# Token-major products that run from the last column to the first, with the split weights at a place that differs by chunk

## The chip, the core and the metric

One core of a Trainium2 chip runs the whole kernel in one launch. The metric is the device time in microseconds (us); the times shown are medians over runs of the same program on the same kind of core. The profile is that of one execution.

## What is computed

One decoder layer on 256 tokens of width 2048, in float32. Cut to what matters here:

```
proj = h @ w_in[l]                            # 2048 x 6144: q, k, v of 8 + 8 heads
a_out = diff_attention(q_d, k_d, v_d, ...)    # 8 heads
b_out = moba_attention(q_m, k_m, v_m, ...)    # 8 heads
mix = concatenate([a_out, b_out]) @ w_out[l]  # 2048 x 2048
h = layer_norm(DEEPNORM_ALPHA * h + mix, ...)
u = h @ w_up                                  # 2048 x 11264: gate and value
f = (silu(causal_dwconv3(gate)) * value) @ w_down   # 5632 x 2048
h = layer_norm(DEEPNORM_ALPHA * h + f, ...)
```

Nearly all of the arithmetic is in the products with the four weight matrices.

## The kernel before, in words

**Three products for one.** TensorE multiplies in a reduced float32 form (`F32R`). To keep the precision, every operand is split into a part `hi`, the value rounded to that form, and a part `lo`, the rest. A product is then hi x hi + hi x lo + lo x hi. ScalarE (ACT) writes `hi` and VectorE (DVE) subtracts to get `lo`: `split` (line 165), `split_hi` and `split_lo` (lines 187 and 197), `split_first` (line 203).

**Two directions.** A matmul holds a stationary operand of 128 x 128 in the array and streams a moving operand of up to 512 columns past it, into one of eight banks of 512 float32 columns. In the *feature-major* products (queries, keys, gate and value; `mm_feature`, line 284, and `up_products`, line 1291) the weights are stationary, and the activations move: 512 columns, hi and lo of 256 tokens, against the `hi` weights, then 256 columns against the `lo` weights. In the *token-major* products (values, output projection, down projection) 128 tokens of the activations are stationary and 512 columns of the weights move, three products for each. These are `mm_token` (line 298), `mm_count` (line 718), through which `mm_d`, `mm_pair`, `mm_three` and the products of `down_products` go, and `mm_d_end` (line 1537), with 256 columns.

**Where the moving operands lie.** The weights come in chunks of 128 x 2048, listed in `stream` and numbered by `i`: 16 of kind "v" (values), 32 of "q" and "k", 16 of "o" (output projection), 88 of "g" and "u" (gate and value), and some of "d" (down projection). Each is loaded by DMA some chunks ahead, and each half of it (1024 columns) is split into one tile `hi` and one tile `lo` of the pool `splits`, six buffers each. Such a tile has 1088 columns, of which 1024 are used. For "v", "o", "d" and the first gate and value chunk, the used part begins 8 columns (32 bytes) into the tile, and for the others at 0: the constant `MOVE_AT`. As the program lays out memory, these tiles begin 96 bytes into a block of 256 bytes, so that the used part begins at 128 with the shift, and at 96 without. The other large operands begin at 128: the activations `x` and `h` in split form, the attention's outputs `mh` and `ml`, and the tiles of block sums named below. One small tile, `hl`, begins at 0.

**Chunks with seven products.** Some chunks are multiplied by a scheme that needs seven block products and some block sums in place of eight (`mm_seven`, line 747). Its operands are sums of blocks of weights in tiles with fixed places: `vhi` and `vlo`, `oslot`, `slot`, and for the early part of the down projection `tslot` and `rslot`, with sums of activations as stationary operands (`wh`, `wl`, `hh`, `hl`, `sp`, `more`, `back`).

**The order.** It is written out by hand. TensorE goes through the chunks; while it works on chunk i, ACT and DVE split chunk i+2, and SP issues the load of a chunk five or six further on. In the stage of gate and value, products of the down projection are put between the chunks (`up_step`, line 1375: `up_products`, then the work of ACT and DVE, then a slice of `down_products`). The value projection takes the first 90 us, queries, keys and attention go to 296, the output projection to 400, gate, value and early down products to 1054, and the remaining down projection and the last norm to the end.

Of the kernel before, what the change touches and what calls it, by code (L numbers as in the profile page):

```python
# [12 lines left out]
F32R = mybir.dt.float32r  # L13
# [3 lines left out]
P = 128  # L17
# [41 lines left out]
MOVE_AT = 8  # L59
# [3 lines left out]
def hymba_layer(ctx: ExitStack, tc: tile.TileContext, a: dict):  # L63
# [3 lines left out]
    def pool(name, bufs=1, space=None):  # L67
        kw = {} if space is None else {"space": space}
        return ctx.enter_context(tc.tile_pool(name=name, bufs=bufs, **kw))

    keep = pool("keep")
    splits = pool("splits", 6)
# [8 lines left out]
    loaded, parts, waiting = {}, {}, {}  # L81

    stream = []
# [23 lines left out]
    first_u = next(i for i, s in enumerate(stream) if s[0] == "g")  # L107
    first_d = next(i for i, s in enumerate(stream) if s[0] == "d")

    def pieces(i, half=None):  # L110

        cuts = [0, 2048] if half is None and stream[i][0] != "v" else [0, 1024, 2048]
        both = [(x, y) for x, y in zip(cuts, cuts[1:])]
        return [p for p in both if half is None or p[0] // 1024 == half]

    def rows_of(p, x, y):
        return 2 * p + x // 512, 2 * p + y // 512
# [42 lines left out]
    def by_dma(i, half):  # L160

        kind, h, _, _ = stream[i]
        return kind == "k" and h < NDIFF and half == 1

    def split(i, half, both=None):

        if i >= NS or (i, half) in parts:
            return
        t = loaded[i] if half == 0 else loaded.pop(i)
        if both is None:  # L170
            o = MOVE_AT if stream[i][0] in "vod" or i - first_u in (0, 1) else 0
            hi, lo = (splits.tile([P, 1088], F32R, name=n)[:, o:o + 1024] for n in ("hi", "lo"))
        else:
            hi, lo = both[:, half], both[:, 2 + half]
        for x, y in pieces(i, half):
            if stream[i][0] == "v" and stream[i][2] == half == 0:
                split_x(*rows_of(stream[i][1], x, y))
            s = slice(x - 1024 * half, y - 1024 * half)
            if by_dma(i, half):
                ACT.activation(lo[:, s], t[:, x:y], AF.Copy, scale=-1.0)  # L180
                POOL.dma_start(lo[:, s], t[:, x:y], accum_op=ALU.add)
            ACT.activation(hi[:, s], t[:, x:y], AF.Copy)  # L182
            if not by_dma(i, half):
                DVE.tensor_tensor(lo[:, s], t[:, x:y], hi[:, s].bitcast(F32), ALU.subtract)  # L184
        parts[i, half] = (hi, lo)

    def split_hi(i, half):
        if i >= NS or (i, half) in parts:
            return
        o = MOVE_AT if stream[i][0] in "vod" or i - first_u in (0, 1) else 0  # L190
        hi, lo = (splits.tile([P, 1088], F32R, name=n)[:, o:o + 1024] for n in ("hi", "lo"))
        t = loaded[i] if half == 0 else loaded.pop(i)
        ACT.activation(hi, t[:, half * 1024:half * 1024 + 1024], AF.Copy)  # L193
        parts[i, half] = (hi, lo)
        waiting[i, half] = t
# [7 lines left out]
    def split_first(i):  # L203

        t = loaded.pop(i)
        for c in range(2):
            parts[i, c] = tuple(splits.tile([P, 1088], F32R, name=n)[:, MOVE_AT:MOVE_AT + 1024] for n in ("hi", "lo"))
        for k in range(2):
            split_x(2 * i + k, 2 * i + k + 1)
            for c in range(2):  # L210
                hi, lo = (x[:, k * 512:k * 512 + 512] for x in parts[i, c])
                src = t[:, c * 1024 + k * 512:c * 1024 + k * 512 + 512]
                ACT.activation(hi, src, AF.Copy)  # L213
                DVE.tensor_tensor(lo, src, hi.bitcast(F32), ALU.subtract)

    def weights(i, x, w):

        hi, lo = parts[i, x // 1024]
        return hi[:, x % 1024:x % 1024 + w], lo[:, x % 1024:x % 1024 + w]
# [11 lines left out]
    def split_x(k0, k1):  # L231
        t = xraw[:, k0 * S:k1 * S].rearrange("p (k t) -> p k t", t=S)
        ACT.activation(xh[:, k0:k1], t, AF.Copy)
        DVE.tensor_tensor(xl[:, k0:k1], t, xh[:, k0:k1].bitcast(F32), ALU.subtract)
# [46 lines left out]
    def mm(out, lhsT, rhs, start, stop):  # L281
        PE.matmul(out, lhsT, rhs, start=start, stop=stop)  # L282
# [14 lines left out]

    def mm_token(dst, i, x, ah, al, first, last):

        w = [weights(i, x + c * 512, 512) for c in range(len(dst))]  # L300
        for c, d in enumerate(dst):
            mm(d, ah, w[c][0], first, False)
        for c, d in enumerate(dst):
            mm(d, ah, w[c][1], False, False)
        for c, d in enumerate(dst):
            mm(d, al, w[c][0], False, last)


    heads = {}
# [404 lines left out]
    MB = {1: bank[4], 5: bank[5], 6: bank[6], 7: bank[7]}  # L714
    MO = ({1: bank[7], 5: bank[5], 6: bank[6], 7: bank[4]}, {1: bank[3], 5: bank[0], 6: bank[2], 7: bank[1]})
    counts, total = {}, {}

    def mm_count(key, dst, lhs, rhs):

        n = counts[key] = counts.get(key, 0) + 1  # L720
        if key in total:
            mm(dst, lhs, rhs, n == 1, n == total[key])

    def mm_three(key, dst, lhs, rhs):
        for x, y in ((0, 0), (0, 1), (1, 0)):
            mm_count(key, dst, lhs[x], rhs[y])

    def mm_d(i, t, cs, k):

        kind, _, n, _ = stream[i]  # L730
        ts = slice(t * P, (t + 1) * P)
        ah, al = (x[:, ts] for x in aparts[i, k])
        w = [weights(i, 1024 * c + 512 * k if kind == "v" else (1536 * c if k == 0 else 512 + 512 * c), 512) for c in cs]
        for lhs, j in ((ah, 0), (ah, 1), (al, 0)):
            for c, wc in zip(cs, w):
                mm_count((kind, n, t, c), CB[t][c], lhs, wc[j])
# [171 lines left out]
    for i in range(2):  # L908
        split_first(i)
        load(4 + i)  # L910
    split(2, 0)

    def begin(i):

        urgent(i)
        j = i + 2
        if j < NS and seven(j):
            blocks_raw(j)
            act_sums(j)
        elif j - 1 < NS and seven(j - 1):  # L920
            blocks_sum(j - 1, 1)
            if j - 1 >= VP:
                split(j, 1)
            blocks_hi(j - 1, 1)
            if j - 1 < VP:
                blocks_whole(j - 1)
                blocks_lo(j - 1, 3)
            else:
                blocks_lo(j - 1, 3)
                blocks_whole(j - 1)  # L930
            if j - 1 < VP:
                split(j, 0)
                split(j, 1)
        else:
            split(j, 0)
            split(j, 1)
        if i >= first_d:
            act_back(i + 3)
        load(i + 6)
        pending(i)  # L940
# [138 lines left out]
    def mm_o(i, kk, t):  # L1079
        _, half, j, _ = stream[i]  # L1080
        ts = slice(t * P, (t + 1) * P)
        h = 2 * j + kk
        mm_token(bank[4 * half + 2 * t:4 * half + 2 * t + 2], i, kk * 1024, head(0, h)[:, ts], head(1, h)[:, ts],
                 h == 0, h == NH - 1)

    def mm_o_columns(i, t, c):
        _, half, j, _ = stream[i]
        ts = slice(t * P, (t + 1) * P)
        for kk in range(2):
            h = 2 * j + kk  # L1090
            mm_token([bank[4 * half + 2 * t + c]], i, (kk * 2 + c) * 512, head(0, h)[:, ts], head(1, h)[:, ts],
                     h == 0, h == NH - 1)
# [17 lines left out]
    last = range(first_u - PAIRED, first_u)  # L1110
    for i in range(first_o, last[0]):
# [23 lines left out]
        n, j = stream[i][1:3]  # L1135
# [239 lines left out]
    def up_step(i):  # L1375
# [25 lines left out]
        if carried:  # L1401
            carried.pop()()
        split_hi(i + 2, 0)
        behind = 0 <= turning < SEGMENTS - 1 and step == 3
        if 2 in now and behind:
# [23 lines left out]
        if 0 in new:  # L1429
            s_lo(1)  # L1430
        split_hi(i + 2, 1)
        if behind:
            up_copy(i)
# [96 lines left out]
    last = range(NS - PAIRED_END, NS)  # L1530
# [6 lines left out]
    def mm_d_end(j):  # L1537

        for i in last:
            for k in range(2):  # L1540
                wh, wl = weights(i, 1536 - 512 * k + j * 256, 256)
                ah, al = (x[:, P:2 * P] for x in aparts[i, k])
                dst = MB[5 + j][:, 0:256]
                mm(dst, ah, wh, i == last[0] and k == 0, False)
                mm(dst, ah, wl, False, False)
                mm(dst, al, wh, False, i == last[-1] and k == 1)
# [3 lines left out]
    for i in range(first_d, NS - PAIRED_END):  # L1550
        begin(i)
        _, p, n, j = stream[i]
# [102 lines left out]
    for j in range(2):  # L1655
        mm_d_end(j)
        z_piece(1, 6 + j, MB[5 + j][:, 0:256], 2, 256, 1.0)
        if j == 0:
            z_times_g(1)
# [94 lines left out]
```

## Time and profile before

| | us |
|---|---|
| median of 3 runs | 1105.75 (1105.56 to 1106.29) |
| span of the profiled execution, first to last instruction | 1104.2 |
| TensorE busy with products (PE) | 1094.6, 5884 products |
| TensorE busy with loading stationary operands (PEld) | 943.7 |
| VectorE (DVE) | 947.3 |
| ScalarE (ACT) | 720.5 |
| GpSimd (POOL) | 71.6 |

The profile gives the span of its execution and no other time for it; the median lies 1.55 us above this span. "Line 282" is the helper through which all products go, so the groups are told apart by the names in them: `bank<-hi,x` has the moving operand `hi` and the stationary operand `x`, and `bank<-x,hi` the other way about. Products overlap: one that lasts 390 ns in a row can be followed by the next after 227 ns, and the distance between starts is the one that adds up to the span.

### The profile page before, as it was taken

The page shows a single profiled execution, that of the slowest core. Times are in us where ns is not written, and L with a number is a line of the kernel's source. Part 1 is how long each engine was busy: PE and PEld are TensorE (multiplying, and loading weights), DVE is VectorE, ACT ScalarE, POOL GpSimd, SP SyncE. Part 2 cuts the span into 40 slices and gives each one's busy share as a digit, 9 for nine tenths or more (in the row PEclk, how much of TensorE's full clock was granted, in tenths as well). Part 3 has the DMA queues.
Part 4 walks back from the last instruction along what each step waited for, and adds up shares of the span by engine and source line. Part 5 has one row for each costly group of instructions (what it writes and reads, how often), then busy time and mean ns, then how long its engine had stood idle before and what let it go on. Part 6 is the DMA issues. An engine that isn't in the chain of part 4 may idle for free.

```text
span 1104.2 us, 16138 instructions
## 1 busy us (share of the span) xinstructions
PE 1094.6 (99%) x5884; PEld 943.7 (85%) x5884; DVE 947.3 (86%) x1613; ACT 720.5 (65%) x1166; POOL 71.6 (6%) x99
## 2 busy tenths in 40 slices
PE   9999999999999999999999999999999999999997
PEld 6888888888888898888888888888888888888886
DVE  6987778888789879888999989998899988998776
ACT  6765676655475386666667767676776767677652
POOL 0100110000000000000000000000100000000003
PEclk9999999999999999999999999999999999999999
DMA  9799876444468647888888889889888889888672
GB/s 338 262 284 304 259 214 209 155 153 153 163 200 260 226 151 233 288 274 270 311 276 285 296 283 326 298 311 308 280 271 280 306 309 300 302 278 282 205 293 77
DMA packets 64336, 283.54 MB, mean 257 GB/s; under 512 B 6576, under 2 KB 8064, under 8 KB 46464
## 3 DMA queue, kind: packets, MB, share of 16 engines
q1 hardware_dynamic: 53456, 235.57, 57.5%
q0 software_dynamic: 10656, 46.67, 19.0%
q8 instruction: 46, 0.75, 0.3%
q14 instruction: 34, 0.28, 0.1%
q10 hardware_dynamic: 144, 0.26, 0.1%
HBM read 233.69 MB, written 20.97 MB: 231 GB/s over the span
## 4 chain that ended last, share of the span: by engine, by line
PE 94%; DVE 3%; ACT 1%; issue 0%; DMA 0%; SPq 0%; POOL 0%; ACTq 0%; DVEq 0%
PE bank L282 94%; PE bank L428 0%; DMA raw<-in_w_v 0%; DVE lo L201 0%; DVE tslot L844 0%; ACT tslot L841 0%; DVE z L1365 0%; ACT hi L193 0%; DVE z L1150 0%; ACT rslot L1514 0%; DVE st L499 0%; DVE rslot L1516 0%; PE bank L1159 0%; PE bank L475 0%; DVE z L496 0%
## 5 line engine op out<-in xcount | busy, mean ns | idle before, releaser
L282 PE MATMUL bank<-h,hi 128*128 128x512 f32 x1376 | 481.0, 390 | 0.2 <-ACT ub L1279 0.2
L282 PE MATMUL bank<-h,lo 128*128 128x256 f32 x1376 | 387.9, 282 | 0.0
L282 PEld LDWEIGHTS bank<-h,hi 128*128 128x128 f32 x1376 | 258.3, 188 | 55.1 <-ACT ub L1279 0.6
L282 PEld LDWEIGHTS bank<-h,lo 128*128 128x128 f32 x1376 | 260.0, 189 | 3.6
L201 DVE TENSOR_TENSOR lo<-raw,hi 128x1024 fp32r<-128x1024 f32 x171 | 208.2, 1220 | 16.1 <-ACT hi L193 15.9
L282 PE MATMUL bank<-x,hi 128*128 128x512 f32 x512 | 182.9, 398 | 0.0
L193 ACT ACTIVATE hi<-raw 128x1024 fp32r<-128x1024 f32 x171 | 178.6, 1048 | 0.0
L184 DVE TENSOR_TENSOR lo<-raw,hi 128x1024 fp32r<-128x1024 f32 x117 | 140.0, 1221 | 41.5 <-ACT hi L182 41.1
L182 ACT ACTIVATE hi<-raw 128x1024 fp32r<-128x1024 f32 x125 | 129.7, 1055 | 46.3 <-PE bank L282 25.9
L282 PE MATMUL bank<-x,lo 128*128 128x256 f32 x512 | 144.2, 282 | 0.0
L841 ACT ACTIVATE tslot<-tf 128x512 fp32r<-128x512 f32 x144 | 88.4, 627 | 62.6 <-DVE tf L1460 23.1
L282 PEld LDWEIGHTS bank<-x,hi 128*128 128x128 f32 x512 | 96.2, 188 | 20.6 <-issue 1.0
L844 DVE TENSOR_TENSOR tslot<-tf,tslot 128x512 fp32r<-128x512 f32 x144 | 97.5, 688 | 11.1 <-ACT tslot L841 10.6
L1279 ACT ACTIVATE ub<-bank 128x512 f32<-128x512 f32 x86 | 50.8, 590 | 73.0 <-PE bank L282 73.0
L282 PEld LDWEIGHTS bank<-x,lo 128*128 128x128 f32 x512 | 96.8, 189 | 0.2
L282 PE MATMUL bank<-hi,x 128*128 128x512 f32 x192 | 51.6, 390 | 0.6 <-ACT hi L213 0.6
L282 PE MATMUL bank<-tslot,more 128*128 128x512 f32 x192 | 49.1, 391 | 0.0
L1288 DVE TENSOR_TENSOR ub<-ub 128x256 f32<-128x256 f32 x86 | 36.2, 421 | 12.5 <-ACT ub L1279 12.5
L1417 POOL DMA_DIRECT2D rslot<-raw x18 | 15.8, 879 | 466.8 <-ACT sp L847 466.8
L282 PE MATMUL bank<-tslot,sp 128*128 128x512 f32 x180 | 45.0, 391 | 0.0
L282 PEld LDWEIGHTS bank<-hi,x 128*128 128x128 f32 x192 | 35.9, 188 | 8.8 <-ACT hi L213 1.5
L562 ACT ACTIVATE gc<-ub,vec 128x256 f32<-128x256 f32 x43 | 25.7, 597 | 26.4 <-DVE ub L1288 26.4
(277 smaller groups left out, 1660.5 us busy)
## 6 DMA issues: line engine op xcount, KB each, us to landing
raw<-in_w_u SPq DMA_DIRECT2D x88, 1024.0 KB, 6.7
raw<-in_w_qk SPq DMA_DIRECT2D x32, 1024.0 KB, 5.0
raw<-in_w_d SPq DMA_DIRECT2D x52, 512.0 KB, 6.1
ring<-in_w_d SPq DMA_DIRECT2D x36, 512.0 KB, 6.2
raw<-in_w_o SPq DMA_DIRECT2D x16, 1024.0 KB, 5.0
raw<-in_w_v SPq DMA_DIRECT2D x28, 512.0 KB, 7.1
rslot<-raw POOLq DMA_DIRECT2D x18, 768.0 KB, 7.0
dparts<-rslot SPq DMA_DIRECT2D x20, 512.0 KB, 8.6
```

The costliest lines, as they stand in the source:

```text
L182: ACT.activation(hi[:, s], t[:, x:y], AF.Copy)
L184: DVE.tensor_tensor(lo[:, s], t[:, x:y], hi[:, s].bitcast(F32), ALU.subtract)
L193: ACT.activation(hi, t[:, half * 1024:half * 1024 + 1024], AF.Copy)
L201: DVE.tensor_tensor(lo, t[:, half * 1024:half * 1024 + 1024], hi.bitcast(F32), ALU.subtract)
L282: PE.matmul(out, lhsT, rhs, start=start, stop=stop)
L562: ACT.activation(gates[f], g, AF.Identity, bias=vec[:, C_CB + f:C_CB + f + 1], scale=vec[:, C_W + 2 * FT + f:C_W + 2 * FT + f + 1])
L841: ACT.activation(side["t"][:, 0, j], f, AF.Copy)
L844: DVE.tensor_tensor(side["t"][:, 1, j], f, side["t"][:, 0, j].bitcast(F32), ALU.subtract)
L1279: ACT.activation(t.rearrange("p j t -> p (j t)"), up_bank(i), AF.Copy)
L1288: DVE.tensor_tensor(u[:, 0], u[:, 0], u[:, 1], ALU.add)
L1417: POOL.dma_start(side["r"][:, 1], w[:, 0:3], accum_op=ALU.add)
```

## The change

The token-major products, all that go through `mm_token`, `mm_count` and `mm_d_end`, now take the columns of the moving operand with a step of -1 and write the columns of the bank with a step of -1, so that each sum still lands in the same column. Feature-major products, the products of the attention and `mm_first` (the first gate and value chunk) keep their order. The shift of the used part inside the tiles `hi` and `lo` becomes 8 x (i mod 8) columns for "v", "o" and "d", that is 0, 32, 64, ... 224 bytes by the chunk's number; the first gate and value chunk keeps 8 columns, the rest 0. In the built program the instructions of every engine stand in the same order as before, and a few waits are written at other instructions.

```
+    def move_at(i):
+        if i - first_u in (0, 1):
+            return MOVE_AT
+        return MOVE_AT * (i % 8) if stream[i][0] in "vod" else 0
...
-            o = MOVE_AT if stream[i][0] in "vod" or i - first_u in (0, 1) else 0
+            o = move_at(i)
             hi, lo = (splits.tile([P, 1088], F32R, name=n)[:, o:o + 1024] for n in ("hi", "lo"))
...
-        w = [weights(i, x + c * 512, 512) for c in range(len(dst))]
+        w = [[y[:, ::-1] for y in weights(i, x + c * 512, 512)] for c in range(len(dst))]
         for c, d in enumerate(dst):
-            mm(d, ah, w[c][0], first, False)
+            mm(d[:, ::-1], ah, w[c][0], first, False)
...
         if key in total:
-            mm(dst, lhs, rhs, n == 1, n == total[key])
+            mm(dst[:, ::-1], lhs, rhs[:, ::-1], n == 1, n == total[key])
...
-                wh, wl = weights(i, 1536 - 512 * k + j * 256, 256)
+                wh, wl = (y[:, ::-1] for y in weights(i, 1536 - 512 * k + j * 256, 256))
...
-                dst = MB[5 + j][:, 0:256]
+                dst = MB[5 + j][:, 255::-1]
```

The other two products of `mm_token` are changed as the first is, and `split_hi` and `split_first` take the place from `move_at` as well.

More of the change, by code (lines that the diff above doesn't have):

```diff
@@ L189, in split_hi @@
             return
-        o = MOVE_AT if stream[i][0] in "vod" or i - first_u in (0, 1) else 0
+        o = move_at(i)
         hi, lo = (splits.tile([P, 1088], F32R, name=n)[:, o:o + 1024] for n in ("hi", "lo"))
@@ L206, in split_first @@
         for c in range(2):
-            parts[i, c] = tuple(splits.tile([P, 1088], F32R, name=n)[:, MOVE_AT:MOVE_AT + 1024] for n in ("hi", "lo"))
+            o = move_at(i)
+            parts[i, c] = tuple(splits.tile([P, 1088], F32R, name=n)[:, o:o + 1024] for n in ("hi", "lo"))
         for k in range(2):
@@ L298, in mm_token @@
     def mm_token(dst, i, x, ah, al, first, last):
-        w = [weights(i, x + c * 512, 512) for c in range(len(dst))]
+        w = [[y[:, ::-1] for y in weights(i, x + c * 512, 512)] for c in range(len(dst))]
         for c, d in enumerate(dst):
-            mm(d, ah, w[c][0], first, False)
+            mm(d[:, ::-1], ah, w[c][0], first, False)
         for c, d in enumerate(dst):
-            mm(d, ah, w[c][1], False, False)
+            mm(d[:, ::-1], ah, w[c][1], False, False)
         for c, d in enumerate(dst):
-            mm(d, al, w[c][0], False, last)
+            mm(d[:, ::-1], al, w[c][0], False, last)
     heads = {}
```

## The prediction

> **What bounds the kernel now.** I read the page first, then the table by stages, then TensorE's instructions in order of time in three short stretches, then one tile. The page's busy times, the chain of waits and the costliest groups:
>
> ```profile
> PE 1094.6 (99%) x5884; PEld 943.7 (85%) x5884; DVE 947.3 (86%) x1613; ACT 720.5 (65%) x1166; POOL 71.6 (6%) x99
> ...
> PE 94%; DVE 3%; ACT 1%; issue 0%; DMA 0%; SPq 0%; POOL 0%; ACTq 0%; DVEq 0%
> ...
> L282 PE MATMUL bank<-h,hi 128*128 128x512 f32 x1376 | 481.0, 390 | 0.2 <-ACT ub L1279 0.2
> L282 PE MATMUL bank<-h,lo 128*128 128x256 f32 x1376 | 387.9, 282 | 0.0
> ...
> L282 PE MATMUL bank<-x,hi 128*128 128x512 f32 x512 | 182.9, 398 | 0.0
> ```
>
> TensorE is busy for 1094.6 of 1104.2 us and is 94% of the chain that ended last; idle time before its products is 0.2 us or less in these groups. By stages (value projection; query, key and attention; output projection; up and early down products; the rest; the columns are length, busy us with counts of PE, PEld, DVE, ACT and POOL, then TensorE's granted clock, DMA share, GB/s):
>
> ```profile
> 0.00:90.40 90.40, 88.61 (x382) 71.14 (x383) 73.60 (x111) 62.11 (x85) 5.77 (x11) 1.00 0.87 283
> 90.40:295.80 205.40, 205.28 (x1247) 181.51 (x1246) 164.01 (x366) 122.50 (x273) 11.84 (x15) 1.00 0.63 207
> 295.80:399.80 104.00, 103.29 (x523) 87.83 (x522) 90.61 (x148) 61.28 (x98) 4.13 (x5) 1.00 0.57 188
> 399.80:1054.00 654.20, 653.98 (x3529) 567.77 (x3528) 582.90 (x931) 457.89 (x689) 40.76 (x60) 1.00 0.86 287
> 1054.00:1104.00 50.00, 43.46 (x210) 35.49 (x208) 36.15 (x59) 16.73 (x22) 9.13 (x8) 0.96 0.44 165
> ```
>
> No stage but the last leaves TensorE idle for over 2 us, and the clock is whole. So what a product takes from its start to the next one's start is what the kernel's time is made of. The mean in a group (390 ns) is a pipelined product's own length, not that distance; the distance is read from starts. A stretch of token-major products (start, length, form, count):
>
> ```profile
> 40.75 1.07 PE L282 MATMUL bank<-hi,x 128*128 128x512 f32 x4
> 41.66 0.62 PE L282 MATMUL bank<-lo,x 128*128 128x512 f32 x2
> 42.11 1.07 PE L282 MATMUL bank<-hi,x 128*128 128x512 f32 x4
> ```
>
> Six products between 40.75 and 42.11 us: 1.36 us / 6 = 226.7 ns each. Token-major products of 256 columns, near the end:
>
> ```profile
> 1092.18 0.28 PE L282 MATMUL bank<-lo,back 128*128 128x256 f32 x1
> ...
> 1092.30 0.40 PE L282 MATMUL bank<-hi,back 128*128 128x256 f32 x2
> ...
> 1092.54 0.28 PE L282 MATMUL bank<-lo,back 128*128 128x256 f32 x1
> ```
>
> Three in 0.36 us: 120 ns each. So 256 columns more take 106.7 ns, 0.417 ns a column; 512 columns take 213.3 ns, and a fixed 13.3 ns is left over in each product (120 - 106.7 gives the same). The feature-major products, which the change doesn't touch, for comparison:
>
> ```profile
> 590.16 0.39 PE L282 MATMUL bank<-h,hi 128*128 128x512 f32 x1
> 590.39 0.28 PE L282 MATMUL bank<-h,lo 128*128 128x256 f32 x1
> ...
> 592.94 0.39 PE L282 MATMUL bank<-h,hi 128*128 128x512 f32 x1
> ```
>
> Eight pairs (hi and lo) lie between 590.16 and 592.94: 347 ns a pair, 320 ns of them columns, so 13.5 ns fixed in each as well. Their stationary operand starts 96 bytes into a 256-byte block and their moving operand 128; in the token-major products both start at 128, which is what the constant 8 (32 bytes) does for the tiles hi and lo. Two different relations of the two addresses, one fixed part.
>
> **What the change can touch.** In the built program 1719 of the 5884 products get both the moving operand and the bank with a step of -1: 1671 of 512 columns and 48 of 256. No instruction changes place on any engine, none is added, and the sizes of tiles and transfers stay. The terms:
>
> 1. *The columns.* 1671 x 213.3 + 48 x 106.7 = 361.5 us of the span are their column time. If a backward step goes at one column per 0.417 ns, as a forward one does, this term is 0. No row shows a backward step; the bounds are 0 and a halved rate, +361.5 us. I take 0: the same columns of the same blocks are visited, only in the other order.
>
> 2. *The fixed part.* 1719 x 13.3 = 22.9 us. While a product runs, the stationary operand of the next is already loaded: PEld is busy 943.7 us beside PE's 1094.6. If the 13.3 ns come from the two reads meeting in the memory, the direction of one of them can change how often they meet. The bounds: all of it goes, -22.9 us; or more meetings. That addresses can add time, one tile shows. These are products of the output projection with block sums, with the shortest, middle and longest duration of each form:
>
> ```profile
> L282 PE MATMUL bank<-oslot,mh x18: 389/389/390, 317.0 to 360.8; 128*128 128x512 f32 x18
> L282 PE MATMUL bank<-oslot,hh x12: 389/395/396, 314.9 to 358.0; 128*128 128x512 f32 x12
> L282 PE MATMUL bank<-oslot,wl x6: 389/389/389, 316.7 to 361.7; 128*128 128x512 f32 x6
> L282 PE MATMUL bank<-oslot,hl x6: 397/397/397, 315.4 to 358.3; 128*128 128x512 f32 x6
> ```
>
> The tile hl starts at a multiple of 256 bytes where mh, hh and wl start 128 bytes past one. All six products with it take 397 ns and not 389, and of those with hh, some of which run while hl is loaded, at least half take 395 or more. So 6 to 8 ns is what a disagreeing address costs here, in a product whose work is otherwise the same. It is paid when the place changes from one product to the next; the feature-major pairs, whose places disagree all the time, pay nothing beyond the fixed 13.5. I take this for the change too: the direction alone, the same in a run of products, 0.
>
> 3. *The places.* Chunks of "v", "o" and "d" now have hi and lo at 32 x (i mod 8) bytes past the tile's start, before always at 32. Of 756 products that read these tiles, 96 keep their place (i mod 8 is 1) and 660 move. Inside a chunk the place is constant; by term 2 the price falls due when a chunk with another place begins. 31 chunks run so, and two products at each entry at 8 ns make 31 x 2 x 8 = 0.5 us. The bounds: 0, and 8 ns in all 660, 5.3 us. I take 0.5.
>
> 4. *ACT and DVE, which write at the new places.* ACT's and DVE's splits run with the place 0 and with 32 bytes today:
>
> ```profile
> L193 ACT ACTIVATE hi<-raw x171: 1041/1047/1061, 403.1 to 1042.6; 128x1024 fp32r<-128x1024 f32 x171
> L201 DVE TENSOR_TENSOR lo<-raw,hi x171: 1216/1219/1227, 404.8 to 1044.3; 128x1024 fp32r<-128x1024 f32 x171
> L182 ACT ACTIVATE hi<-raw x125: 1039/1053/1083, 13.7 to 1068.0; 128x1024 fp32r<-128x1024 f32 x125
> L184 DVE TENSOR_TENSOR lo<-raw,hi x117: 1209/1220/1227, 14.8 to 1069.2; 128x1024 fp32r<-128x1024 f32 x117
> ```
>
> Lines 193 and 201 write at place 0 only; 182 and 184 mix both, and the middle values agree within 6 ns. Six more places of the same kind: 0, with cover from TensorE's queue of products, which is what ends everything. Without that cover 6 ns in some 60 splits would be 0.4 us.
>
> 5. *Waits.* A few waits are written elsewhere: DVE's sum of bank 6 at line 1310 (three times) now waits for the third product into that bank itself, and ACT's copy from a bank at line 1101 and its copy into bank 3 at line 1633 name one more engine. Behind DVE's sum stand the sum into ring, line 1356, and the next step's splits, for which TensorE waits. What it now names is over: ACT's copy of bank 6 (line 1334), which reads the same sum, stands ahead of the splits of blocks that DVE has waited for by then. In the two other cases the wait is on what the reader's own product or sum has waited for. 0; had DVE to stand for three products each time it would be 3 x 0.68 = 2 us of DVE, of whose lateness TensorE shows at most 0.2 us before any group above.
>
> The sum: 0 + 0 + 0.5 + 0 + 0 on a span of 1104.2 us gives 1104.7. The median of the runs is 1105.75, 1.55 above the span, so I forecast **1106.3 us**. That is within 0.2% (2.2 us), about the least that a measurement of this kernel can tell from no change. 2.2 us are 1.3 ns in each of the 1719 products: the result stays inside only if neither direction nor place changes the usual product at all.
>
> The Trainium skill, page "TensorE: Matmul & The Clock Gate", Part 2 (What happens when you issue a matmul), says that TensorE has two independent read ports, so that loading the next weights takes no read bandwidth from the running product. By that rule direction and place would both cost nothing, and the time would be 1105.75. The row of hl speaks against it as a whole: 8 ns hang on an address alone.
>
> **The rivals.**
>
> *Fewer meetings: faster.* If the 13.3 ns are the two reads crossing each other, and both now run the same way, part of it goes. For it: an address effect exists, TensorE has no other slack, and the gain needs no other engine. Against it: two relations of addresses have the same 13.3 to 13.5 ns, as a plain cost per product would. Its price by the one step that an address makes in this trace, 8 ns: 1719 x 8 = 13.8 us, 1092.0; its end, all 13.3 ns, 1082.9. The same page, Back-to-back issue gap, gives 2.5 ns over the columns for an isolated stream; by it, an estimate, 10.8 ns would go in each, which is 1087.2, and no run here shows such a gap.
>
> *The place decides in every product: slower.* Moving and stationary operands in token-major products agree today at 128 bytes; the moved 660 no longer do. If the 8 ns of hl fall due in every such product and not only at the change, this is +5.3 us, 1111.0; if a backward start counts as a disagreeing place too, all 1719 pay, +13.8 us, 1119.5. It decides from 3.3 ns in each of the 660 (2.2 us). For it: hl pays in all of its products. Against it: the feature-major pairs.
>
> *Backward steps break the access: much slower.* If the bank or the moving operand then goes at half rate, term 1's other end: 1467. For it there is no row; against it that every pair of neighbours is still a pair. The Trainium skill, page "PSUM — Partial Sum Buffer", Specifications, says that any access that is not contiguous slows matmuls significantly, with lines of 8 bytes; whether a descending run counts as contiguous it doesn't say, and no run here shows it.
>
> **How the numbers follow.** Forecast 40%, fewer meetings 27%, places 28%, half rate 5%. The range reaches from 1086, which holds most of the first rival (5 of its 27 left out below), to 1113, which holds the second at its 660 products and leaves out its dearer end (8%) and the half rate (5%): 18% left out. The forecast's own range is 1104 to 1108. Faster by over 0.2%: 0.27; within: 0.40; slower: 0.33.
>
> **What would show it.** Right: token-major products still start 226.7 ns apart (six in 1.36 us near 41 us), their groups keep 389 to 391 ns, and a step of 8 ns shows only at a chunk's first products. The first rival: distances of 213 to 220 ns in all reversed products, tslot and rslot too, with the feature-major pairs at 347. The second: groups of hi and lo at 395 to 398 and, by chunk, a pattern with i mod 8, with the tiles of fixed place at 389. The third: lengths of 600 ns. I am wrong at the root if TensorE shows idle time before its products that it does not have now.

## The result, and the profile after

| | before | after |
|---|---|---|
| median, us | 1105.76 (1105.56 to 1106.29, 4 runs) | 1115.91 (1115.34 to 1116.07, 4 runs) |
| span of the profiled execution, us | 1104.2 | 1114.3 |
| PE busy, us | 1094.6 | 1105.4 |

The ratio is 1.0086 (95% interval 1.0073 to 1.01): 10.15 us slower. The forecast was 1106.3 and the range ended at 1113, so both missed.

The rows of the page of after that answer to those of before: busy times, the chain of waits, and groups (line 288 is now the helper of all products; busy us and mean ns stand behind the bar, idle us before the group behind the second one):

```profile
PE 1105.4 (99%) x5884; PEld 945.0 (85%) x5884; DVE 947.9 (85%) x1613; ACT 720.7 (65%) x1166; POOL 71.5 (6%) x99
...
PE 95%; DVE 2%; ACT 1%; DMA 1%; issue 0%; ACTq 0%; DVEq 0%
...
L288 PE MATMUL bank<-h,hi 128*128 128x512 f32 x1376 | 481.4, 391 | 0.2 <-ACT ub L1285 0.2
...
L206 DVE TENSOR_TENSOR lo<-raw,hi 128x1024 fp32r<-128x1024 f32 x171 | 208.2, 1220 | 17.5 <-ACT hi L198 17.3
...
L198 ACT ACTIVATE hi<-raw 128x1024 fp32r<-128x1024 f32 x171 | 178.5, 1047 | 0.0
...
L288 PE MATMUL bank<-hi,x 128*128 128x512 f32 x192 | 53.6, 403 | 0.0
L288 PE MATMUL bank<-tslot,more 128*128 128x512 f32 x192 | 50.0, 397 | 0.0
...
L288 PE MATMUL bank<-tslot,sp 128*128 128x512 f32 x180 | 45.9, 397 | 0.0
```

PE's busy time grew by 10.8 us, the other engines' by under 1.4, and no product waits longer than before. The groups with reversed columns are longer, `tslot` and `hi` alike, and the feature-major `h,hi` has 391 ns for 390. The stages again, of which two rows are shown: the value projection, in the same 90.4 us as before, and gate and value with the early down products, cut at 400 and 1060 us:

```profile
0.00:90.40 90.40, 89.21 (x371) 69.94 (x372) 72.26 (x110) 60.48 (x83) 5.78 (x11) 1.00 0.85 279
...
400.00:1060.00 660.00, 659.76 (x3556) 570.40 (x3555) 585.62 (x934) 459.27 (x694) 38.62 (x56) 1.00 0.84 282
```

The clock is whole, and in the first 90.4 us TensorE now gets through 371 products instead of 382, and is no less busy (89.21 us, before 88.61). In the later row it is busy for all but 0.24 us. The stretch of token-major products near 41 us, in order of time:

```profile
40.48 1.10 PE L288 MATMUL bank<-hi,x 128*128 128x512 f32 x4
41.41 0.63 PE L288 MATMUL bank<-lo,x 128*128 128x512 f32 x2
41.88 1.10 PE L288 MATMUL bank<-hi,x 128*128 128x512 f32 x4
```

Six products take 1.40 us where they took 1.36: 233.3 ns each for 226.7. Over the whole trace, leaving out the 12 products with a wait behind them, 1659 reversed products of 512 columns went from a mean of 227.64 to 233.46 ns, start to start: 1659 x 5.82 = 9.65 us. The 48 of 256 columns gave back 0.07, and the other 4164 distances added 0.57: together 10.15 us. The mean is below 6.6 because 204 of them had been above 230 ns already: 79 that stand just ahead of a feature-major product (235.0 ns each), and among the others the products of the tile `hl`. The rows of the products of `oslot`, three forms shown, now read (shortest, middle, longest ns):

```profile
L288 PE MATMUL bank<-oslot,mh x18: 397/397/398, 320.0 to 365.1; 128*128 128x512 f32 x18
L288 PE MATMUL bank<-oslot,hh x12: 396/398/400, 317.9 to 362.3; 128*128 128x512 f32 x12
...
L288 PE MATMUL bank<-oslot,hl x6: 395/398/400, 318.4 to 362.6; 128*128 128x512 f32 x6
```

`mh` has come up from 389 to where `hl` was before and still is. `oslot` has a fixed place, so the new places cannot be the reason here.

### The profile page after: what moved, and what is told of

Read it like the earlier page. It is cut to its first block, busy times and chain, and to the rows that moved or that the text cites. A ratio compares the mean times of both kernels' runs of the same rounds, so it can differ in the third digit from the quotient of the medians.

```text
span 1114.3 us, 16138 instructions
## 1 busy us (share of the span) xinstructions
PE 1105.4 (99%) x5884; PEld 945.0 (85%) x5884; DVE 947.9 (85%) x1613; ACT 720.7 (65%) x1166; POOL 71.5 (6%) x99
## 4 chain that ended last, share of the span: by engine, by line
PE 95%; DVE 2%; ACT 1%; DMA 1%; issue 0%; ACTq 0%; DVEq 0%
PE bank L288 95%; DMA raw<-in_w_d 1%; PE bank L434 0%; DVE lo L206 0%; PE bank L1165 0%; ACT hi L198 0%; ACT rslot L1520 0%; PE bank L481 0%; ACT tslot L847 0%; DVE z L1608 0%; DVE z L1371 0%; DVE tf L1458 0%; ACT rslot L1422 0%; DVE z L1604 0%; DVE h L1180 0%
## 5 line engine op out<-in xcount | busy, mean ns | idle before, releaser
L206 DVE TENSOR_TENSOR lo<-raw,hi 128x1024 fp32r<-128x1024 f32 x171 | 208.2, 1220 | 17.5 <-ACT hi L198 17.3
L198 ACT ACTIVATE hi<-raw 128x1024 fp32r<-128x1024 f32 x171 | 178.5, 1047 | 0.0
L1294 DVE TENSOR_TENSOR ub<-ub 128x256 f32<-128x256 f32 x86 | 36.2, 421 | 13.5 <-ACT ub L1285 13.3
```

The lines of the kernel that those rows point to most:

```text
L206: DVE.tensor_tensor(lo, t[:, half * 1024:half * 1024 + 1024], hi.bitcast(F32), ALU.subtract)
L1294: DVE.tensor_tensor(u[:, 0], u[:, 0], u[:, 1], ALU.add)
```

## The experiments

The theory after the result: reading the moving operand backward puts a higher fixed part on each product of 512 columns. Rivals: the new places do it; the backward writing of the bank does it; or the direction matters only through the place where a read starts.

### The parts of the change alone

The direction alone, with the place of before (the edit is to the changed kernel):

```
     def move_at(i):
...
-        return MOVE_AT * (i % 8) if stream[i][0] in "vod" else 0
+        return MOVE_AT if stream[i][0] in "vod" else 0
```

> The changed kernel with the old place (32 bytes for every chunk of v, o and d): the direction alone. Theory A, each product that runs backward pays a longer fixed part (20.0 ns in place of 13.3, as the 233.3 ns between starts in the changed kernel's trace read): 1719 x 6.5 ns, about 1115 to 1116 us, starts of 512-column products 233.3 ns apart. Theory B, the places by chunk cost it: 1105.8 us, starts 226.7 ns apart.

Measured: 1115.15 us (1114.80 to 1115.44), ratio 1.0084 [1.0067, 1.0101]. 1617 of the 1671 reversed distances are 232 to 235 ns. The direction accounts for 9.4 of the 10.15 us. Rows of its page:

```profile
L288 PE MATMUL bank<-hi,x 128*128 128x512 f32 x192 | 53.2, 400 | 0.0
L288 PE MATMUL bank<-tslot,more 128*128 128x512 f32 x192 | 50.0, 397 | 0.0
```

Before, both groups lay at 390 and 391 ns.

The places alone, all columns forward as in the kernel before:

```
+    def move_at(i):
+        if i - first_u in (0, 1):
+            return MOVE_AT
+        return MOVE_AT * (i % 8) if stream[i][0] in "vod" else 0
...
-            o = MOVE_AT if stream[i][0] in "vod" or i - first_u in (0, 1) else 0
+            o = move_at(i)
```

> The kernel before with the new places by chunk, all products forward. Theory A (direction alone): 1105.8 us, up to 0.5 more for the changes of place, starts 226.7 ns apart at every place. Theory B (a place that disagrees with the stationary operand's costs 6 to 8 ns a product): 660 products, 1110 to 1111 us, starts of 233 to 235 ns in the moved chunks.

Measured: 1109.73 us (1109.58 to 1109.93), ratio 1.0035 [1.0022, 1.0048], 4.0 us over before. Rows of its page:

```profile
L288 PE MATMUL bank<-hi,x 128*128 128x512 f32 x192 | 52.6, 395 | 0.7 <-ACT hi L219 0.7
L288 PE MATMUL bank<-tslot,more 128*128 128x512 f32 x192 | 49.1, 391 | 0.0
```

`hi` went from 390 to 395 ns; `tslot`, of fixed place, stayed at 391. The mean distances of 512-column products with `hi` or `lo`, by where the moving operand starts in its block of 256 bytes (the stationary operand starts at 128):

| start | 128 | 0 | 32 | 64 | 96 | 160 | 192 | 224 |
|---|---|---|---|---|---|---|---|---|
| ns | 227.6 | 232.4 | 233.9 | 233.5 | 233.3 | 233.3 | 229.4 | 234.1 |

So a place is paid for in every product of a chunk, by 2 to 6.5 ns, and not when it changes. The two parts don't add: 9.4 + 4.0 is 13.4, and both together cost 10.15. Read backward, a product is at 233 ns already with the place of before, and most other places can't make it dearer.

### Reading and writing apart

Only the moving operand backward, and only the bank backward; the columns of the products concerned land mirrored:

```
-            mm(dst, lhs, rhs, n == 1, n == total[key])
+            mm(dst, lhs, rhs[:, ::-1], n == 1, n == total[key])
```

```
-            mm(dst, lhs, rhs, n == 1, n == total[key])
+            mm(dst[:, ::-1], lhs, rhs, n == 1, n == total[key])
```

and likewise in `mm_token` and `mm_d_end`, at the place of before.

> Old place; the moving operand is read backward, the bank is written forward, so the columns of every token-major product land mirrored in their block. Theory A1, the backward read pays: 1115 to 1116 us and 233.3 ns between starts. Theory A2, the backward write of the bank pays: 1105.8 us and 226.7 ns.

> Old place; the moving operand is read forward, the bank is written backward, so the columns land mirrored. Theory A1 (the read pays): 1105.8 us and 226.7 ns between starts. Theory A2 (the write pays): 1115 to 1116 us and 233.3 ns.

Measured: reading backward 1115.32 us (1115.07 to 1115.38), 1.0085 [1.007, 1.01]; writing backward 1105.77 us (1105.63 to 1106.31), 1.0 [0.999, 1.0009]. The same products in order of time, reading backward:

```profile
40.42 1.10 PE L288 MATMUL bank<-hi,x 128*128 128x512 f32 x4
41.36 0.63 PE L288 MATMUL bank<-lo,x 128*128 128x512 f32 x2
41.82 1.10 PE L288 MATMUL bank<-hi,x 128*128 128x512 f32 x4
```

and writing backward:

```profile
40.85 1.07 PE L288 MATMUL bank<-hi,x 128*128 128x512 f32 x4
41.75 0.62 PE L288 MATMUL bank<-lo,x 128*128 128x512 f32 x2
42.21 0.84 PE L288 MATMUL bank<-hi,x 128*128 128x512 f32 x3
```

Six products in 1.40 and in 1.36 us. The read costs all of it, the write nothing. The Trainium skill, page "PSUM — Partial Sum Buffer", Specifications, has it that any access that is not contiguous slows matmuls significantly; a descending run is not such an access, by these runs.

### The products by themselves

Series of 24 products on zeros were put ahead of the kernel before, other engines idle, with one stationary operand `W`; `there` and `back` give the moving operand forward and backward. They change the direction, the place of the moving operand (in columns of 4 bytes from the agreeing one), the width and the number format, and some products stand alone.

```
+    for _ in range(24): PE.matmul(bank[6][:, 0:512], W, there(pf, 512, 0), start=True, stop=True)
...
+    for _ in range(24): PE.matmul(bank[6][:, 0:512], W, back(pf, 512, 0), start=True, stop=True)
```

> The kernel before with some 900 extra products on zeros put ahead of its work, 24 of a kind in a row while the other engines are idle; its time is not compared. Read: the distance between starts of float32 products of 512 columns, forward and backward, with the moving operand 0, 4, 8, 16, 32, 64, 128 and 192 bytes away from the stationary operand's place in a 256-byte block; of 128, 256 and 384 columns; of bfloat16; and the length of single products that run alone, with no stationary operand being loaded beside them. Theory L (the load of the next stationary operand costs it): forward at 0 has 226.7 ns, forward elsewhere 230 to 234, backward 233 wherever it lies, and single products last as long backward as forward. Theory P (a backward product is longer by itself): single backward products last 6 to 7 ns longer than forward ones.

Rows in order of time; each line of code is one series (921 forward at 0 columns, 925 forward at 8, 929 backward at 0, 946 to 948 bfloat16 forward at 0, at 16 and backward, 952 and 962 single float32 products forward and backward):

```profile
11.33 5.60 PE L921 MATMUL bank<-pf 128*128 128x512 f32 x24
16.77 5.84 PE L922 MATMUL bank<-pf 128*128 128x512 f32 x24
...
33.59 5.76 PE L925 MATMUL bank<-pf 128*128 128x512 f32 x24
39.20 5.66 PE L926 MATMUL bank<-pf 128*128 128x512 f32 x24
...
55.86 5.76 PE L929 MATMUL bank<-pf 128*128 128x512 f32 x24
61.46 0.87 PE L930 MATMUL bank<-pf 128*128 128x512 f32 x3
```

```profile
135.24 5.34 PE L947 MATMUL bank<-pb 128*128 128x512 bf16 x24
140.42 5.34 PE L948 MATMUL bank<-pb 128*128 128x512 bf16 x23
...
151.50 0.50 PE L952 MATMUL bank<-pf 128*128 128x512 f32 x1 [0.26 <-DVE mx L950]
...
176.64 0.50 PE L962 MATMUL bank<-pf 128*128 128x512 f32 x1 [0.25 <-DVE mx L960]
```

From a series' start to the next one's, by 24: forward 5.44 / 24 = 226.7, at 8 columns 5.61 / 24 = 233.8, backward 5.60 / 24 = 233.3 ns. Over all eight places tried, forward reads 226.7 to 236.7 and backward 233.3 to 236.7, so the bounds of theory L (230 to 234, and 233 backward) were too narrow. The kernel's two values come back without changing weights, and but for the first two series no DMA, ACT or DVE ran beside these. In bfloat16 direction and place cost nothing: 215.8 ns in all three series, the columns and 2.5 ns. The Trainium skill, page "TensorE: Matmul & The Clock Gate", section Back-to-back issue gap, gives the same 2.5 ns. For float32 the fixed part is 13.3 or 20.0 ns. A product that stands alone takes 497 to 505 ns forward (six of them) and 501 to 502 backward (the first four; the last two, 777 and 792 ns, fell in a stretch with a granted clock of 0.89): no direction shows, and theory P falls. The surcharge showed only in a stream. It depends on the width too: backward 118.5 ns against 119.4 at 256 columns, 177.8 against 173.4 at 384, 233.3 against 226.7 at 512.

So theory L was kept, and the texts that follow call it L too: in a float32 stream the stationary operand of the next product is read beside the moving operand of the running one, and the extra nanoseconds are the two reads meeting.

### The feature-major products

Their moving operand and bank reversed in place of the token-major ones; and, the other way, all chunks at the place of the token-major ones, which makes moving and stationary operand of the feature-major products agree:

```
-            mm(dst, wh, t2[:, k].rearrange("p j t -> p (j t)"), k == 0, False)
+            mm(dst[:, ::-1], wh, t2[:, k].rearrange("p j t -> p (j t)")[:, ::-1], k == 0, False)
```

and likewise for the product with `wl`, and in `up_products`;

```
-            o = MOVE_AT if stream[i][0] in "vod" or i - first_u in (0, 1) else 0
+            o = MOVE_AT
```

> The kernel before with the feature-major products backward (moving operand and bank), the token-major ones forward as they were: 1888 products of 512 columns and 1888 of 256, whose moving and stationary places disagree already (128 and 96). Theory L (backward is one more way of not agreeing with the stationary load): nothing is added, pairs stay at 347 ns, 1105.8 us within 1. Theory P (6.5 ns for each backward product of 512 columns): 1888 x 6.5 ns, 1118 us, pairs at 353 ns.

> The kernel before, all forward, with hi and lo of every chunk at 32 bytes, so that the feature-major products agree as well (stationary and moving both at 128). If disagreeing adds time to feature-major products too, their pairs fall from 347 ns to at least 340, 1888 x 6.5 ns, down to 1093.5 us. If their pairs of 512 and 256 columns come to the same either way, only the 20 ns at each change between the two directions goes (79 steps): 1104.1 us.

Measured: feature-major backward 1115.56 us (1115.49 to 1116.10), 1.0088 [1.0071, 1.0105]; all places agreeing 1116.26 us (1116.15 to 1116.41), 1.0093 [1.0078, 1.0108]; the kernel before, run beside them, 1106.06. Products near 590 us in order of time, feature-major backward:

```profile
589.92 0.40 PE L282 MATMUL bank<-h,hi 128*128 128x512 f32 x1
590.16 0.28 PE L282 MATMUL bank<-h,lo 128*128 128x256 f32 x1
590.27 0.40 PE L282 MATMUL bank<-h,hi 128*128 128x512 f32 x1
```

and with agreeing places:

```profile
589.78 0.40 PE L282 MATMUL bank<-h,hi 128*128 128x512 f32 x1
...
590.14 0.40 PE L282 MATMUL bank<-h,hi 128*128 128x512 f32 x1
...
590.49 0.40 PE L282 MATMUL bank<-h,hi 128*128 128x512 f32 x1
...
590.84 0.40 PE L282 MATMUL bank<-h,hi 128*128 128x512 f32 x1
```

Backward, inside a chunk, the product of 512 columns takes 233.3 ns from start to start (228.4 before) and the one of 256 columns about 118, as before; a pair is about 351 for 347. Over the whole trace the 1888 products of 512 columns account for 8.5 of the 9.6 us by which it grew. So the direction costs here too, 4.8 ns a product inside a chunk, in products whose places had not agreed. Neither expected time came out: L as I had put it, with nothing to lose where the places don't agree, fell, and P's 1118 us were too many. The agreeing places were the surprise: 1.06 us for three pairs, 353 ns each, where both of the expected numbers lay below the kernel before. What made the feature-major pairs cheap before was not that place is indifferent to them. In order of time the pairs repeat 349, 350 and 361 ns, in threes, on through the chunks of 16. The expected 340 is there, but in the first pair of a step alone: 72 of the 80 first pairs that nothing holds up take 339 or 340 ns, and the next one is mostly back at 350.

### Places, one by one

Series of 20 as above (`mov(n, o, back)` gives n columns of the moving operand from place o on, backward with True): forward at each of the 64 places in a block of 256 bytes, backward at every third, with 64 and 32 stationary columns, and pairs of 512 and 256 columns over 20 places of the stationary operand.

```
+    for _ in range(20): PE.matmul(bank[6], pf[:, 0:P], mov(512, 1), start=True, stop=True)
...
+    for _ in range(20): PE.matmul(bank[6][0:64], pf[:, 0:64], mov(512, 0, True), start=True, stop=True)
```

> As the first probe, some 2700 extra products on zeros ahead of the work; its time is not compared. Read: forward products with the moving operand at each of the 64 columns of a 256-byte block from the stationary operand's place, backward ones at every third; products whose stationary operand has 64 or 32 columns; and pairs of 512 and 256 columns as in the feature-major products, by the stationary operand's place. Theory L (the load of the next stationary operand costs the time beyond the columns): the 32 cycles over 512 columns (226.7 ns) and the 48 (233.3 ns) shrink with the columns loaded, to about 220 and 223 ns with 64, and forward and backward come together. Theory N (it is the streams of neighbouring products, not the load): 64 and 32 columns keep 226.7 and 233.3 ns. No place is expected under 226.7 ns; if one is, the kernel can use it.

Rows in order of time (979 forward at 63 columns, 980 backward at 0, 1002 and 1005 forward and backward with 64 stationary columns):

```profile
305.11 4.71 PE L979 MATMUL bank<-pf 128*128 128x512 f32 x20
309.65 4.83 PE L980 MATMUL bank<-pf 128*128 128x512 f32 x20
...
413.48 4.76 PE L1002 MATMUL bank<-pf 128*64 128x512 f32 x20
...
427.32 4.83 PE L1005 MATMUL bank<-pf 128*64 128x512 f32 x20
```

Measured, ns from start to start without a series' first four (means of 15 distances, which swing by several ns at some places): forward 226.67 at 6 places of 64 (0, 7, 15, 27, 39 and 63 columns), up to 240.0 at the dearest, 233.3 typical. Backward 233.2 to 241.3, 226.7 nowhere. The backward series at 0 reads its first column at the same byte of a block as the forward series at 63 columns, a cheap place, and still takes 233.3: it is not the place where a backward read starts. Stationary operands of 64 and 32 columns, whose loads take 135 and 108 ns instead of 188, don't bring back 226.7: forward is dearer than with 128 columns at place 0 (229.9 and 231.8 ns) and a little cheaper at 8 and 48 (231.1 to 232.0), and backward stays at 233.33. Theory L's 220 and 223 did not come, so a shorter load doesn't take the surcharge away. Pairs run from 346.3 (place 0) to 353.3 ns (places 16, 28, 48 and 60); the kernel's own place, 8 columns short, has 347.2. So the feature-major pairs of before sit at one of the cheap places, which are 7 of the 20 tried (346.3 to 347.3 ns).

### Both operands moved

More questions in series of 20: the stationary operand at 32 places with the moving one fixed, in both directions; both moved together; the moving one some KB further on; two kinds in turn.

```
+    for _ in range(20): PE.matmul(bank[6], pf[:, 1024 + 8:1024 + 8 + P], mov(512, 0, True), start=True, stop=True)
...
+    for _ in range(20): PE.matmul(bank[6], pf[:, 1024 + 16:1024 + 16 + P], mov(512, 16), start=True, stop=True)
...
+    for _ in range(20): PE.matmul(bank[6], pf[:, 0:P], mov(512, 0, _ % 2 == 1), start=True, stop=True)
```

> Series of 20 products on zeros ahead of the kernel before, one after the other, the other engines idle; its total time is not compared. Read are distances from start to start of float32 products of 512 columns. (a) moving operand at 0, stationary operand at 32 even places from 0 to 62 columns, forward and backward; (b) both operands moved together by 1 to 49 columns, forward; (c) moving operand 2, 4 and 6 KB further on; (d) two moving operands in turn: two blocks, two places, two directions. Theory R (the two operands' places relative to each other decide): forward runs from 226.7 to 236 or more over the stationary operand's places; moved together every series reads 226.7; and backward, where only the relation has changed, some stationary place brings 226.7 to 228 back. Theory A (the moving operand's own place or direction decides, wherever the stationary operand lies): forward reads 226.7 at every stationary place, moved together reads what the place alone read (231 at 4 columns, 233 at 8, 229 at 16, 232 at 32), and backward reads 233.2 or more at every stationary place. In both, a series in which two kinds take turns reads the mean of the two kinds (230.0 forward and backward in turn); theory N (the step from one product's last address to the next one's first decides) gives for those a value outside the two, and another one than 226.7 for two blocks in turn.

Rows in order of time (916 forward, both at 0; 920 the stationary operand at 8 columns; 956 backward with it at 16; 983 both at 16, forward; 996 two blocks in turn; 999 forward and backward in turn):

```profile
11.63 4.70 PE L916 MATMUL bank<-pf 128*128 128x512 f32 x20
...
30.05 4.83 PE L920 MATMUL bank<-pf 128*128 128x512 f32 x20
...
197.46 4.83 PE L956 MATMUL bank<-pf 128*128 128x512 f32 x20
...
323.58 4.72 PE L983 MATMUL bank<-pf 128*128 128x512 f32 x20
...
383.84 4.71 PE L996 MATMUL bank<-pf 128*128 128x512 f32 x20
...
397.66 4.89 PE L999 MATMUL bank<-pf 128*128 128x512 f32 x20
```

In these rows 4.70 to 4.72 us is the cheap value for 20 products, 4.83 the dear one. Without the first four, moving only the stationary operand costs forward what moving the other one did (233.2 at 8 columns; 226.67 again at two of 32 places, 0 and 30). Moved together by 8, 16, 32 or 48 columns the products are cheap again, 226.9 to 227.5, though the moving operand's place by itself had read 233.4, 228.9, 232.4 and 233.3: for these shifts the relation of the two places decides, as R has it, and A falls. But not every series moved together is cheap, as R expected: by odd numbers of columns (1, 25, 33, 49) it is 237.7 to 237.8, by 4 columns 231.1 and by 30 columns 233.3, so the relation is not all. The moving operand 2, 4 and 6 KB further on changes little: 226.7 to 227.5 forward, 233.3 backward. Backward it is 233.2 to 233.5 at 30 of the 32 stationary places and 236.6 or more at two: none brings 226.7 back, against R's expectation. Two blocks in turn read 226.67, where N expected another value; places 0 and 8 in turn 231.6 (mean of the two 230.0), 0 and 16 in turn 231.8 (mean 227.8); forward and backward in turn 236.9, dearer than either. N's expectation came out in the last two alone, but in three of the four the mean is missed: a product's price depends on its neighbours.

### Mixed streams

Float32 products of 512 columns (forward at 0, at 8 columns, backward) in turn with bfloat16 products, three to one, and in turn with float32 products of 128 columns (`one(t, n, o, back)` is one product; `pf` is float32, `pb` bfloat16):

```
+    for _ in range(24): one(pf, 512, 0, True) if _ % 2 else one(pb, 128, 0)
...
+    for _ in range(24): one(pf, 512, 0, True) if _ % 4 else one(pb, 128, 0)
```

> Series on zeros ahead of the kernel before, the other engines idle; its total time is not compared. Float32 products of 512 columns, forward at place 0, forward at 8 columns and backward, stand alone in a series, in turn with bfloat16 products of 128 and of 512 columns, three to one with bfloat16 products of 128 columns, and in turn with float32 products of 128 columns. Read is the time of a pair (or of a group of four), start to start. Theory L (the dear value comes where the stationary operand of a following float32 product is loaded beside the float32 stream): in turn with bfloat16 the three kinds differ by under 1 ns a pair, since a bfloat16 operand is loaded beside the float32 stream and the float32 one beside the bfloat16 stream; three to one, two of the three float32 products have a float32 load beside them, and backward is dearer by 2 x 6.6 = 13 ns in the group; in turn with float32 products of 128 columns backward is dearer by about 6.6. Theory S (the float32 stream itself takes longer backward or at a disagreeing place, whatever is loaded beside it): 6.6 ns a pair in turn with bfloat16 too, and 20 ns in the group of four.

| ns for a pair or group | forward, 0 | forward, 8 | backward |
|---|---|---|---|
| with bfloat16 of 128 columns | 358.9 | 359.7 | 359.9 |
| with bfloat16 of 512 columns | 460.0 | 460.1 | 464.3 |
| three, and one bfloat16 of 128 | 826.8 | 823.5 | 827.8 |
| with float32 of 128 columns | 340.0 | not tried | 348.4 |

L's 13 ns in the group of four did not appear (1.0), nor did the 20 of S; in turn with bfloat16 of 128 columns backward is 1.0 dearer, not S's 6.6. In turn with bfloat16 of 512 columns it is 4.3 dearer, where L allowed 1 and S asked 6.6, and with float32 of 128 columns 8.4, a little over L's 6.6. Between bfloat16 products the forward series loses its advantage: within a group of four its float32 products start 231 and 238 ns apart. So neither theory stands as a price per product.

What the experiments bear out: 233.3 ns is what a float32 product of 512 columns in an uninterrupted stream usually takes, and 226.7 a favourable case that needs a forward read, a good relation of the two operands' places, and neighbours of the same kind. The change takes the first of these away. Why the read's direction matters is open: that the reads of the two operands meet is argued from the relation of the places, and a narrower load, which should then cost less, left backward at 233.33 ns. The trace of before has a point on either side. All 85 token-major products of 512 columns whose successor's stationary operand starts elsewhere than at 128 in its block (79 at 96, 6 at 0) are dear, 235.0 and 232.3 ns, and only 119 of the other 1574; but the six products of `hl` are dear too (234.3 ns), whose successors' stationary operands start at 128. The direction of the stationary operand was not tried.

## Why the prediction was wrong

**Term 1, the columns: right as far as it goes.** Nothing like a halved rate appeared (the reversed distances grew by 2.6%), and the write order is free (1105.77).

**Term 2, the fixed part: the step that failed.** It took "the direction alone, the same in a run of products, 0". Measured: 5.82 ns in each of 1659 products, 9.65 us; with the direction alone the kernel is 9.4 us slower. The working went wrong in one inference. It saw that `hl` costs 8 ns in all of its products, saw feature-major pairs with another relation of places at the same 13.5 ns, and concluded that only a change of place is paid for. A change does cost (the 79 products ahead of feature-major ones), but so does a place or a direction that never changes. Two relations of places were too few: in the series both of the kernel's are cheap for their kind (226.67 ns for products of 512 columns, 347.2 for pairs), where most are dear. And none of the rows that it drew on read a moving operand backward.

**Term 3, the places: the same premise, hidden by term 2.** It took 31 entries at 16 ns, 0.5 us. Forward, the places cost 4.0 us, 6 ns in each of the 660 moved products. In the changed kernel they add 0.76 us (1115.91 against 1115.15), close to the 0.5 but for another reason: the backward products are at the dear value already. Only the chunks with i mod 8 = 5, whose used part begins at 0 in the block, are dearer: 236.5 ns.

**Terms 4 and 5, ACT, DVE and the waits: right.** The splits keep 1220 and 1047 ns, and no group of TensorE's waits longer than before.

**The rivals.** "The place decides in every product" was nearest, in its dearer form: all 1719 pay, 1119.5. The scope was right (`tslot` and `oslot` pay as `hi` does), which its own forecast of a pattern by i mod 8 with fixed tiles at 389 had excluded. The reason was not: a backward read isn't one more disagreeing place, since no place tried mends it. The size was too high for two reasons: 8 ns is the difference of two lengths in rows (397 and 389), while the starts moved by 6.6; and 204 of the products were dear already. The range left this end out for 8%. "Fewer meetings" looked at the 13.3 ns as slack; no series of float32 products of 512 columns came under 226.67 ns, so no address or direction tried takes any of it away. The gap of 2.5 ns that stands beside this rival shows here in bfloat16 alone (215.8 ns).

**The two read ports.** Two independent read ports, by which direction and place would cost nothing (the Trainium skill, page "TensorE: Matmul & The Clock Gate", Part 2), agree with the bfloat16 series. What the prediction drew from them doesn't hold for float32: 226.7 and 233.3 ns on a place or a direction alone. Whether that comes from the ports is open. Beside it the prediction had the row of `hl`, and followed neither to the end.

No version tried beats the kernel before.

## What to carry to other kernels

When TensorE is the bound, the unit of account is the distance between starts in a stream; 6 ns in a quarter of the products was 0.9% here. By these runs, a stream of float32 products of 512 columns that runs at the cheap value owes it to forward reads and to the places of its tiles, so a change of direction or layout should be priced as losing it, in every product, until a short series on the chip says otherwise. A second group that shows no cost under other conditions is one sample of many and no proof that the conditions don't matter.

## What the runs showed of the hardware

- Float32 products of 512 columns in a stream cost 13.3 ns over the columns at best and usually 20.0; the dearest series read 240.0 ns forward and 241.3 backward. In bfloat16 it is 2.5 in either direction and at the two places tried.
- Of 64 places of the moving operand against a fixed stationary one, 6 read 226.67 ns. Moving both operands by 8, 16, 32 or 48 columns keeps the price (226.9 to 227.5); by 1, 25, 33 or 49 it becomes 237.7 ns. A place 8 columns off costs nothing at 384 columns (173.4 ns either way).
- Backward reading costs 6.6 ns at 512 columns, 4.4 at 384 and nothing at 256 (118.5 against 119.4), and none that shows in a product alone. Backward writing of a bank is free (1105.77 us for 1105.76).
- A float32 product of 128 columns in a stream takes 111.7 ns, twice its columns' 53.3. Float32 and bfloat16 in turn are dear: 358.9 ns for 512 + 128 columns, whose column time is 266.7.
- Left open: with agreeing places the kernel's feature-major pairs take 353 ns, and the same pairs in a series of their own 346.3. There the stationary operand is the same in every pair, in the kernel it moves on by 512 bytes; whether that is the cause was not tried. The pairs' rhythm of three in the kernel runs on over the ends of the chunks, so it doesn't follow the place within a chunk.
